# Tying the large products of a hybrid DeltaNet and mixture-of-experts block in program order, with three smaller moves

## The chip, the cores and the metric

The kernel runs on one core of a Trainium2 chip. The metric is the device time of one launch in microseconds (us). Engines are named as in the profile: PE is TensorE (matmul), PEld its weight load, DVE is VectorE, ACT is ScalarE, POOL is GpSimd, SP is SyncE, which issues nearly all DMA.

## The reference, cut to what matters

One block of a decoder over 512 tokens of width 1024, in float32:

```python
proj = x @ w_in                                  # q, k, v, z, a, b, uv, two gates
q, k, v = split(silu(causal_conv4(qkv)))         # 8 heads of 128; q and k are normalised
beta = sigmoid(b)
g = -exp(a_log) * softplus(a + dt_bias)          # per token and head, summed along the tokens
o = gated_delta_rule(q, k, v, g, beta)           # decay = exp(g_cum differences), triangular solves, state
y_dn  = (rms_norm(o) * silu(z)) @ w_dn_out
y_sgu = (u * (W_causal @ layer_norm(v_sgu) + b)) @ w_sgu_out
y = (sigmoid(gate_dn) * y_dn + sigmoid(gate_sgu) * y_sgu) @ w_out
h = layer_norm(ALPHA * x + y)
# router: the best of 4 groups, 2 of its 4 experts, combine weights
ffn = sum_e combine_e * ((silu(h @ w_gate_e) * (h @ w_up_e)) @ w_down_e)     # 16 experts, FF 256
out = layer_norm(ALPHA * h + ffn)
```

## The kernel before

**Split products.** Nearly every product is made of three: each float32 operand is split into a high half (a copy rounded to float32r, made by ACT) and a low half (what is left, made by DVE with a subtraction that waits for the copy). `mm3` (L235 to L237) issues high x high, high x low, low x high into one PSUM bank, 512 columns each. Three lines are thus the bulk of PE's work: L235, L236 and L237 in the projections, L1202 to L1204 in the experts.

**Blocks.** `chan_tile` makes one block of 24 such products (8 chunks of the contraction by 3) for 128 channels by 512 tokens. `tok_half` makes half a block for 128 tokens by 512 channels. The results lie in PSUM tiles `pa`, of which there are four, taken in turn. The small products (transposes, attention, the state) use four tiles `pb`.

**Weights.** `wload` fetches one MB of weights into one of three raw buffers, lets ACT make the high half (L149) in one of two buffers, and DVE the low half in place of the raw data (L150). One load serves two `chan_tile` blocks.

**The start.** x comes in four pieces; `xturn(k)` transposes chunk k of it on PE (L224 is the warm up, L230 the transposes), ACT writes its high half (L231), DVE its low half (L232). The first half of z's projection is multiplied as x arrives: `z_first(w, kh, m)` does two of the eight chunks for four token tiles. Then come the projections a and b (16 columns), the gates made of them (L323 to L356: Exp, Ln and the cumulative sums on PE, L342 and L343), and the rest of z.

**The heads.** For each of 8 heads of k: a block, a convolution (ACT L384, three DVE steps L386, ACT Silu L387), the small products k k^T (L414), and on DVE their norms (L416) and the matrix A (L400). The decay matrix DM is fetched through DRAM (L363 stores the cumulative gate, L405 reads it back, broadcast), masked by POOL (L425), shifted by DVE (L427) and put through Exp by ACT (L428). Then q with the other half of z, a forward substitution on DVE, v, the recurrence over four chunks of tokens, u, the spatial gate, the merge (L748 to L759), the output projection, the router.

**The experts.** For each expert e the loop does `gate_up(e + 1)` (24 products), the turn of the next tokens (L1180, L1182, L1183), the split of later weights (`esplit`: ACT L809, DVE L813), the transposes of the hidden rows (L1304) with their two halves (ACT L1305, DVE L1307), and `down(e)`. Of the four quarters of `down`, three are made of three split products each. The fourth (n = 1, f = 1) is one product of whole float32 operands: `FHF`, an unsplit copy of the hidden rows made by ACT (L1306), times the unsplit weights (L1224). So the last quarter of each down weight isn't split.

**What sets the order.** A scheduler places the instructions of each engine in a fixed list before the kernel runs. It follows data dependences and, among what it takes for ready, program order; its idea of when something is ready is its own. `K(...)` pins an instruction behind the one traced before it on its engine. `tc.issue_after(ins)` puts those instructions of its block that are on the engine of `ins` behind `ins` in the list; it adds no wait on other engines. The blocks of the projections are not pinned: their products are placed in any order between blocks, though in order within one. The expert loop is pinned throughout. At run time each engine goes through its list in order.

Of the kernel before, what the change touches and what calls it, by code (L numbers as in the profile page):

```python
# [21 lines left out]
NT = 4  # L22
H = 8
KT = 8
# [12 lines left out]
def body(ctx: ExitStack, tc: tile.TileContext, P: dict, out):  # L37
# [161 lines left out]
    xload(2)  # L199
    SP.dma_start(wab, w_in[:, COLS["ab"]:COLS["ab"] + 16].rearrange("(k p) n -> p k n", p=128))  # L200
    fz.append(wfetch(whalf(w_z, 0, 1), 2))
# [32 lines left out]
    def mm3(o, lh, ll, rh, rl, first, last, pin=lambda ins: ins):  # L234
        pin(T.matmul(o, lh, rh, start=first, stop=False))  # L235
        pin(T.matmul(o, lh, rl, start=False, stop=False))  # L236
        pin(T.matmul(o, ll, rh, start=False, stop=last))  # L237

    def chan_tile(w, j, rh=None, rl=None, pin=lambda ins: ins):

        whi, wlo = w
        p = pa()
        for k in range(KT):
            mm3(p, whi[:, k, j * 128:(j + 1) * 128], wlo[:, k, j * 128:(j + 1) * 128],
                XHI[:, k, :] if rh is None else rh(k), XLO[:, k, :] if rl is None else rl(k),
                k == 0, k == KT - 1, pin)
        return p

    def tok_half(p, w, i, kh, lh=None, ll=None, cs=slice(0, 512), pin=lambda ins: ins, ks=range(4)):

        whi, wlo = w
        ts = slice(i * 128, (i + 1) * 128)
        for k in ks:
            mm3(p, (XHI if lh is None else lh)[:, kh * 4 + k, ts], (XLO if ll is None else ll)[:, kh * 4 + k, ts],
                whi[:, k, cs], wlo[:, k, cs], kh + k == 0, kh == 1 and k == 3, pin)
# [22 lines left out]
    def z_first(w, kh, m):  # L278

        for i in range(NT):  # L280
            tok_half(pz[i], w, i, kh, pin=K, ks=range(2 * m, 2 * m + 2))
# [9 lines left out]
    for k in range(4, KT):  # L291
        xturn(k)
    split(wab, wabl, wabh, V, K)
    w = wload(None, fz[1], K)
    z_first(w, 1, 0)
# [32 lines left out]
    A.activation(sl, su, AF.Ln)  # L328
# [16 lines left out]
    for i in range(NT):  # L345
        z_use(0)(i, pz[i])
# [5 lines left out]
    A.activation(Gc, gc, AF.Exp)  # L352
    A.activation(GL, gl, AF.Exp)
    V.tensor_scalar(nG, Gc, -1.0, None, op0=ALU.mult)
    V.tensor_tensor(kd, gl, gc, ALU.subtract)
    A.activation(kd, kd, AF.Exp)  # L356
# [49 lines left out]
    for h in range(H):  # L406
# [15 lines left out]
        if h == 1:  # L422
            for c in range(NT):
                with tc.issue_after(silu.ins):
                    G.affine_select(out=DM[:, c], in_=DM[:, c], compare_op=ALU.is_ge, fill=NEG, base=0,  # L425
                                    pattern=[[0, 8], [1, 128]], channel_multiplier=-1)
                    V.tensor_tensor(DM[:, c], DM[:, c], ngc[:, :, c, None].to_broadcast([128, H, 128]), ALU.add)  # L427
                    A.activation(DM[:, c], DM[:, c], AF.Exp)  # L428
        if h > 1:
            a_matrix(h - 2)  # L430
# [363 lines left out]
    def esplit(n, later=False):  # L794


# [7 lines left out]
        if part < 2:  # L804
            cuts = [lambda t: t[:, 0:2], lambda t: t[:, 2:4]]
        else:
            cuts = [lambda t: t[:, 0], lambda t: t[:, 1, 0:512]]
        for cut in cuts:
            K(A.activation(cut(hi), cut(raw), AF.Copy))  # L809

        def rest():
            for cut in cuts:
                K(V.tensor_tensor(cut(lo), cut(raw), f_(cut(hi)), ALU.subtract))  # L813
# [349 lines left out]
    FHF = cst(128)  # L1163
# [53 lines left out]
    def down(e, n):  # L1217
# [3 lines left out]
        for f in range(2 - n):  # L1221
            kmm3(p, FHH[:, f], FHL[:, f], wh[:, f, ns], wl[:, f, ns], f == 0, f == 1)
        if n == 1:
            K(T.matmul(p, FHF, raws[(e, 2)][0][:, 1, ns], start=False, stop=True))  # L1224
# [68 lines left out]
    for e in range(NE):  # L1293
# [12 lines left out]
        K(A.activation(FHF, p[:, 128:256], AF.Copy))  # L1306
# [125 lines left out]
```

## Time and profile before

| what | us |
|---|---|
| median of 3 runs (lowest, highest) | 836.5 (834.26, 838.26) |
| the profiled execution, its own time | 833.55 |
| its span, from first to last instruction | 831.8 |
| PE busy in the span | 787.8 (95%) |
| DVE, ACT, POOL busy | 522.8, 382.6, 106.1 |
| mean granted clock of PE | 0.978 |

The span is that of one profiled execution; 1.75 us of its time lie outside the span. A matmul's busy time overlaps that of the next one, so the distance between the starts of two matmuls is what one of them costs. Idle time of PE, and time at a granted clock of half, are what can be won on PE.

### The profile page before, as it was taken

Reading aid. Unit: us, or ns where it says so; the run is one execution under the profiler, and the core shown is the slowest. Engines: PE = TensorE matmul, PEld = TensorE weight load, DVE = VectorE, ACT = ScalarE, POOL = GpSimd, SP = SyncE. Lnnn points to the kernel's source line nnn. Section 1 sums busy time; section 2 is a strip of 40 time slices with the busy share of each in tenths; the row PEclk is TensorE's granted clock in tenths of the full one; section 3 lists DMA queues with packets and bytes.
Section 4 is the critical chain, followed back from the end, with each engine's and each line's share of the span. In section 5 each row is a group of like instructions: output and inputs, shape, how many; then the busy total and the mean of one; then the engine's idle time right before and its main releaser. Section 6 shows DMA issues by size and latency. Waiting matters only on the chain. (4 is left out here: it accounts for less than half of the span.)

```text
span 831.8 us, 10884 instructions
## 1 busy us (share of the span) xinstructions
PE 787.8 (95%) x4043; PEld 647.6 (78%) x4043; DVE 522.8 (63%) x1026; ACT 382.6 (46%) x629; POOL 106.1 (13%) x92
## 2 busy tenths in 40 slices
PE   8888999999999999999999999999995999999991
PEld 7577888787889988888788888888664777777771
DVE  3336882997575992447623233324469898889977
ACT  2395353453335543323322222222234888888843
POOL 0002002001100000001501000000032211110177
PEclk9998999999999999999999999999997999999997
DMA  9426336336260135243244333379718899998762
GB/s 223 87 63 157 85 79 142 85 71 153 49 134 2 52 77 100 81 102 97 102 110 98 101 101 102 102 274 335 249 52 267 287 382 390 369 336 294 290 244 101
DMA packets 110752, 133.65 MB, mean 161 GB/s; under 512 B 19780, under 2 KB 93032, under 8 KB 110696
## 3 DMA queue, kind: packets, MB, share of 16 engines
q1 hardware_dynamic: 107240, 120.33, 49.8%
q0 software_dynamic: 3456, 12.58, 4.2%
q8 instruction: 33, 0.54, 0.3%
q14 instruction: 23, 0.19, 0.1%
HBM read 120.82 MB, written 12.08 MB: 160 GB/s over the span
## 5 line engine op out<-in xcount | busy, mean ns | idle before, releaser
L235 PE MATMUL pa<-r,r 128*128 128x512 f32 (+1 forms) x712 | 280.6, 394 | 5.1 <-ACT r L149 4.9
L236 PE MATMUL pa<-r,r 128*128 128x512 f32 (+1 forms) x712 | 279.6, 393 | 2.7 <-DVE r L150 2.7
L237 PE MATMUL pa<-r,r 128*128 128x512 f32 (+1 forms) x712 | 278.5, 392 | 0.0
L150 DVE TENSOR_TENSOR r<-r,r 128x2048 fp32r<-128x2048 f32 (+2 forms) x48 | 102.0, 2131 | 132.4 <-ACT r L149 132.3
L235 PEld LDWEIGHTS pa<-r,r 128*128 128x128 f32 x712 | 134.9, 189 | 32.7 <-ACT r L149 5.7
L236 PEld LDWEIGHTS pa<-r,r 128*128 128x128 f32 x712 | 135.0, 190 | 30.2 <-DVE r L150 3.6
L237 PEld LDWEIGHTS pa<-r,r 128*128 128x128 f32 x712 | 135.2, 190 | 27.8 <-DVE r L232 0.4
L149 ACT ACTIVATE r<-r 128x2048 fp32r<-128x2048 f32 (+2 forms) x48 | 84.8, 1777 | 141.8 <-PE pa L236 83.4
L813 DVE TENSOR_TENSOR r<-r,r 128x1024 fp32r<-128x1024 f32 x96 | 108.8, 1134 | 13.1 <-ACT r L809 11.6
L809 ACT ACTIVATE r<-r 128x1024 fp32r<-128x1024 f32 x96 | 89.2, 983 | 0.0
L1202 PE MATMUL pa<-r,r 128*128 128x512 f32 x176 | 77.3, 439 | 0.3 <-ACT r L1182 0.3
L1204 PE MATMUL pa<-r,r 128*128 128x512 f32 x176 | 69.4, 395 | 0.0
L1203 PE MATMUL pa<-r,r 128*128 128x512 f32 x176 | 69.0, 392 | 0.0
L386 DVE SCALAR_TENSOR_TENSOR r<-pa,r,r 128x511 f32<-128x511 f32 (+2 forms) x72 | 53.5, 743 | 16.7 <-ACT r L384 16.2
L1202 PEld LDWEIGHTS pa<-r,r 128*128 128x128 f32 x176 | 33.1, 188 | 9.3 <-ACT r L809 1.9
L1203 PEld LDWEIGHTS pa<-r,r 128*128 128x128 f32 x176 | 33.2, 189 | 9.0 <-issue 3.1
L1204 PEld LDWEIGHTS pa<-r,r 128*128 128x128 f32 x176 | 33.0, 188 | 7.8 <-DVE r L1307 0.3
L387 ACT ACTIVATE r<-r 128x512 f32<-128x512 f32 x24 | 15.1, 631 | 46.4 <-DVE r L386 42.7
L758 POOL TENSOR_TENSOR r<-r,r 128x512 f32<-128x512 f32 x8 | 12.4, 1556 | 144.0 <-DVE r L757 137.3
L384 ACT ACTIVATE r<-pa,r 128x512 f32<-128x512 f32 x24 | 16.3, 680 | 26.9 <-PE pa L237 26.9
L1040 POOL DMA_INDIRECT r<-hD,r x16 | 17.3, 1080 | 87.7 <-PE pb L1180 45.9
L1182 ACT ACTIVATE r<-pb 128x512 fp32r<-128x512 f32 x32 | 19.1, 599 | 16.0 <-PE pb L1180 14.8
(328 smaller groups left out, 934.2 us busy)
## 6 DMA issues: line engine op xcount, KB each, us to landing
r<-in_w_in_dram SPq DMA_DIRECT2D x29, 1024.0 KB, 8.9
r<-in_expert_w_gate_dram SPq DMA_DIRECT2D x32, 512.0 KB, 5.9
r<-in_expert_w_down_dram SPq DMA_DIRECT2D x16, 1024.0 KB, 10.5
r<-in_expert_w_up_dram SPq DMA_DIRECT2D x32, 512.0 KB, 9.2
yD<-r SPq DMA_DIRECT2D x12, 512.0 KB, 8.7
r<-in_x_dram SPq DMA_DIRECT2D x8, 512.0 KB, 3.7
r<-in_w_dn_out_dram SPq DMA_DIRECT2D x4, 1024.0 KB
r<-in_w_sgu_out_dram SPq DMA_DIRECT2D x4, 1024.0 KB
```

The source lines that it names most:

```text
L149: pin(A.activation(hi, raw, AF.Copy))
L150: pin(eng.tensor_tensor(lo, raw, f_(hi), ALU.subtract))
L235: pin(T.matmul(o, lh, rh, start=first, stop=False))
L236: pin(T.matmul(o, lh, rl, start=False, stop=False))
L237: pin(T.matmul(o, ll, rh, start=False, stop=last))
L386: V.scalar_tensor_tensor(acc[:, s:], p[:, :S - s], wc(3 - s), acc[:, s:], op0=ALU.mult, op1=ALU.add)
L809: K(A.activation(cut(hi), cut(raw), AF.Copy))
L813: K(V.tensor_tensor(cut(lo), cut(raw), f_(cut(hi)), ALU.subtract))
L1182: K(A.activation(XGH[:, hs], v3(p), AF.Copy))
L1202: K(T.matmul(args[0], args[1], args[3], start=args[5], stop=False))
L1203: K(T.matmul(args[0], args[1], args[4], start=False, stop=False))
L1204: K(T.matmul(args[0], args[2], args[3], start=False, stop=args[6]))
```

## The change

Four edits. (1) `mm3` remembers its last product in `big`, and `chan_tile` and `tok_half` put their products behind it, so that the large products of one block follow all those of the block traced before. (2) The start of z: `z_first` runs through its products by term, high x high for all four tiles, then low of x, then low of the weights; its second half is moved ahead of the last two transposed chunks of x; the small load of the weights of a and b goes behind the second piece of z's weights. (3) The four Silu of z are put behind the Ln of the gates, and three Exp of the gates (Gc, GL, kd) move to the block in which DM goes through Exp. (4) The fourth quarter of `down` is made like the other three, so `esplit` splits the whole down weight, and the unsplit copy FHF is gone.

```diff
@@ the loads at the start
     xload(2)
+    fz.append(wfetch(whalf(w_z, 0, 1), 2))
     SP.dma_start(wab, w_in[:, COLS["ab"]:COLS["ab"] + 16].rearrange("(k p) n -> p k n", p=128))
-    fz.append(wfetch(whalf(w_z, 0, 1), 2))
@@ mm3, chan_tile, tok_half
-        pin(T.matmul(o, ll, rh, start=False, stop=last))
+        big[0] = pin(T.matmul(o, ll, rh, start=False, stop=last)).ins
+
+    big = [None]
+
+    def after_big():
+
+        return tc.issue_after(big[0]) if big[0] is not None else contextlib.nullcontext()
...
-        for k in range(KT):
-            mm3(p, whi[:, k, j * 128:(j + 1) * 128], wlo[:, k, j * 128:(j + 1) * 128],
...
+        with after_big():
+            for k in range(KT):
+                mm3(p, whi[:, k, j * 128:(j + 1) * 128], wlo[:, k, j * 128:(j + 1) * 128],
...
-        for k in ks:
-            mm3(p, (XHI if lh is None else lh)[:, kh * 4 + k, ts], (XLO if ll is None else ll)[:, kh * 4 + k, ts],
...
+        with after_big():
+            for k in ks:
+                mm3(p, (XHI if lh is None else lh)[:, kh * 4 + k, ts], (XLO if ll is None else ll)[:, kh * 4 + k, ts],
...
@@ z_first
-        for i in range(NT):
-            tok_half(pz[i], w, i, kh, pin=K, ks=range(2 * m, 2 * m + 2))
+        hi, lo = w
+        terms = ((XHI, hi), (XLO, hi), (XHI, lo))
+        for t, (x, y) in enumerate(terms):
+            for i in range(NT):
+                for k in range(2 * m, 2 * m + 2):
+                    K(T.matmul(pz[i], x[:, kh * 4 + k, i * 128:(i + 1) * 128], y[:, k, 0:512],
+                               start=kh + k + t == 0, stop=False))
@@ the order at the start
     z_first(w, 0, 1)
-    for k in range(4, KT):
+    for k in range(4, 6):
+        xturn(k)
+    w = wload(None, fz[1], K)
+    z_first(w, 1, 0)
+    for k in range(6, KT):
         xturn(k)
     split(wab, wabl, wabh, V, K)
-    w = wload(None, fz[1], K)
-    z_first(w, 1, 0)
     w_k0 = wload(None, f_k0, K)
@@ the gates
-    A.activation(sl, su, AF.Ln)
+    ln_ = A.activation(sl, su, AF.Ln)
...
-    for i in range(NT):
-        z_use(0)(i, pz[i])
+    with tc.issue_after(ln_.ins):
+        for i in range(NT):
+            z_use(0)(i, pz[i])
...
-    A.activation(Gc, gc, AF.Exp)
-    A.activation(GL, gl, AF.Exp)
-    V.tensor_scalar(nG, Gc, -1.0, None, op0=ALU.mult)
     V.tensor_tensor(kd, gl, gc, ALU.subtract)
-    A.activation(kd, kd, AF.Exp)
@@ head 1 of k, behind the Exp of DM
+            with tc.issue_after(silu.ins):
+                A.activation(Gc, gc, AF.Exp)
+                A.activation(GL, gl, AF.Exp)
+                A.activation(kd, kd, AF.Exp)
+                V.tensor_scalar(nG, Gc, -1.0, None, op0=ALU.mult)
@@ esplit
-        if part < 2:
-            cuts = [lambda t: t[:, 0:2], lambda t: t[:, 2:4]]
-        else:
-            cuts = [lambda t: t[:, 0], lambda t: t[:, 1, 0:512]]
-        for cut in cuts:
-            K(A.activation(cut(hi), cut(raw), AF.Copy))
+        halves = (slice(0, 2), slice(2, 4)) if part < 2 else (slice(0, 1), slice(1, 2))
+        for s in halves:
+            K(A.activation(hi[:, s], raw[:, s], AF.Copy))
...
@@ down and the expert loop
-        for f in range(2 - n):
+        for f in range(2):
             kmm3(p, FHH[:, f], FHL[:, f], wh[:, f, ns], wl[:, f, ns], f == 0, f == 1)
-        if n == 1:
-            K(T.matmul(p, FHF, raws[(e, 2)][0][:, 1, ns], start=False, stop=True))
...
         K(A.activation(FHH, v3(p[:, 0:256]), AF.Copy))
-        K(A.activation(FHF, p[:, 128:256], AF.Copy))
```

## Rows read from the trace of the kernel before

**Rows 1.** The page's first two parts: busy time, share of the span and instructions of PE, then the span in 40 equal slices (20.8 us each): busy tenths of PE and DVE, and the granted clock of PE.

```profile
PE 787.8 (95%) x4043; PEld 647.6 (78%) x4043; DVE 522.8 (63%) x1026; ACT 382.6 (46%) x629; POOL 106.1 (13%) x92
PE   8888999999999999999999999999995999999991
DVE  3336882997575992447623233324469898889977
PEclk9998999999999999999999999999997999999997
```

**Rows 2.** Busy time of each engine by stretch (us from the span's start: length, then busy us and instructions of PE, PEld, DVE, ACT, POOL, then granted clock, DMA share, GB/s).

```profile
28.00:55.00 27.00, 27.00 (x117) 19.65 (x118) 6.11 (x19) 15.80 (x23) 0.00 (x0) 0.94 0.24 44
55.00:78.00 23.00, 18.09 (x73) 14.39 (x72) 15.49 (x31) 13.49 (x15) 5.21 (x4) 0.85 0.62 172
78.00:125.00 47.00, 47.00 (x238) 39.39 (x237) 40.60 (x134) 21.41 (x29) 0.00 (x0) 1.00 0.33 80
404.00:560.00 156.00, 156.00 (x690) 129.17 (x689) 51.86 (x43) 40.51 (x38) 15.43 (x10) 1.00 0.43 128
641.00:804.00 163.00, 162.43 (x765) 128.84 (x766) 145.57 (x189) 132.23 (x206) 25.51 (x23) 0.99 0.95 333
```

**Rows 3.** The waits of PE: line that waited, what ended the wait, us in total, times, longest.

```profile
PE pa L235 <- ACT r L149: 4.9, 3, 2.7
PE pa L236 <- DVE r L150: 2.7, 3, 1.1
PE pb L414 <- ACT r L387: 2.2, 1, 2.2
PE pb L488 <- ACT r L387: 1.1, 1, 1.1
```

**Rows 4.** Timeline of PE, and of ACT, in the start (start us, us, engine, line, operation, shapes, count, idle before and its releaser).

```profile
8.92 0.50 PE L235 MATMUL pa<-r,r 128*128 128x512 f32 x1 [0.17 <-ACT r L149]
10.18 0.50 PE L236 MATMUL pa<-r,r 128*128 128x512 f32 x1 [0.76 <-DVE r L150]
22.70 1.91 PE L230 MATMUL pb<-r,r 128*128 128x128 f32 x16
26.59 0.50 PE L235 MATMUL pa<-r,r 128*128 128x512 f32 x1 [1.98 <-ACT r L149]
34.69 0.40 PE L235 MATMUL pb<-r,r 128*16 128x512 f32 x1
23.34 2.06 ACT L231 ACTIVATE r<-pb 128x512 fp32r<-128x512 f32 x4 [6.07 <-PE pb L230]
25.26 4.12 ACT L149 ACTIVATE r<-r 128x128 fp32r<-128x128 f32 x5
```

**Rows 5.** The gates: a transfer of a's products to DVE, the table loads of ACT in 40 to 56 us (grouped by line: count, busy us, mean ns), and PE's product behind z's last ones.

```profile
42.18 0.19 DVE L323 TENSOR_TENSOR r<-pb,r 128x32 f32<-128x32 f32 x1 [10.89 <-PE pb L311]
L273 ACT ACT_TABLE_LOAD x4 | 5.1, 1283 | 0.1
52.23 0.27 PE L359 MATMUL pb<-r,r 128*32 128x128 f32 x1
```

**Rows 6.** The first heads of k, timelines of PE, ACT, DVE and POOL.

```profile
58.51 0.40 PE L236 MATMUL pa<-r,r 128*128 128x512 f32 x1
61.63 0.66 PE L235 MATMUL pa<-r,r 128*128 128x512 f32 x1 [2.72 <-ACT r L149]
71.60 1.70 PE L414 MATMUL pb<-r 128*128 128x128 f32 x8 [2.19 <-ACT r L387]
55.69 1.91 ACT L149 ACTIVATE r<-r 128x2048 fp32r<-128x2048 f32 x1
55.82 2.32 DVE L386 SCALAR_TENSOR_TENSOR r<-pa,r,r 128x511 f32<-128x511 f32 x3 [2.91 <-ACT r L384]
58.05 2.28 DVE L150 TENSOR_TENSOR r<-r,r 128x2048 fp32r<-128x2048 f32 x1
66.32 1.23 DVE L427 TENSOR_TENSOR r<-r,r 128x1024 f32<-128x1024 f32 x1 [5.33 <-POOL r L425]
104.25 2.26 DVE L150 TENSOR_TENSOR r<-r,r 128x2048 fp32r<-128x2048 f32 x1
```

**Rows 7.** Busy time by stretch again, in the heads of k (columns as in rows 2).

```profile
55.80:61.00 5.20, 3.11 (x14) 2.22 (x12) 5.11 (x5) 3.82 (x3) 0.00 (x0) 1.00 0.41 129
66.30:106.50 40.20, 38.01 (x184) 31.59 (x183) 34.84 (x112) 17.67 (x20) 4.11 (x3) 0.96 0.42 104
```

**Rows 8.** One pass of the expert loop: its busy time (columns as in rows 2), then timelines of PE and DVE, and last a group of lines in the experts (count, busy us, mean ns).

```profile
701.52:711.08 9.56, 9.56 (x47) 7.58 (x46) 8.49 (x11) 8.43 (x14) 1.15 (x1) 1.00 1.07 376
700.65 1.02 PE L1224 MATMUL pa<-r,r 128*128 128x512 f32 x2
701.75 0.40 PE L1203 MATMUL pa<-r,r 128*128 128x512 f32 x1
701.41 1.95 DVE L813 TENSOR_TENSOR r<-r,r 128x1024 fp32r<-128x1024 f32 x2
704.33 2.48 DVE L813 TENSOR_TENSOR r<-r,r 128x1024 fp32r<-128x1024 f32 x2 [0.97 <-ACT r L809]
706.73 0.42 DVE L1307 TENSOR_TENSOR r<-pb,r 128x256 fp32r<-128x256 f32 x1
L1234 DVE SCALAR_TENSOR_TENSOR r<-pa,r,r 128x512 fp32r<-128x512 f32 x4 | 2.8, 744 | 0.0
```

More of the change, by code (lines that the diff above doesn't have):

```diff
@@ L1 @@
+import contextlib
 import math
@@ L242, in chan_tile @@
         p = pa()
-        for k in range(KT):
-            mm3(p, whi[:, k, j * 128:(j + 1) * 128], wlo[:, k, j * 128:(j + 1) * 128],
-                XHI[:, k, :] if rh is None else rh(k), XLO[:, k, :] if rl is None else rl(k),
-                k == 0, k == KT - 1, pin)
+        with after_big():
+            for k in range(KT):
+                mm3(p, whi[:, k, j * 128:(j + 1) * 128], wlo[:, k, j * 128:(j + 1) * 128],
+                    XHI[:, k, :] if rh is None else rh(k), XLO[:, k, :] if rl is None else rl(k),
+                    k == 0, k == KT - 1, pin)
         return p
@@ L252, in tok_half @@
         ts = slice(i * 128, (i + 1) * 128)
-        for k in ks:
-            mm3(p, (XHI if lh is None else lh)[:, kh * 4 + k, ts], (XLO if ll is None else ll)[:, kh * 4 + k, ts],
-                whi[:, k, cs], wlo[:, k, cs], kh + k == 0, kh == 1 and k == 3, pin)
+        with after_big():
+            for k in ks:
+                mm3(p, (XHI if lh is None else lh)[:, kh * 4 + k, ts], (XLO if ll is None else ll)[:, kh * 4 + k, ts],
+                    whi[:, k, cs], wlo[:, k, cs], kh + k == 0, kh == 1 and k == 3, pin)
     def tok_group(src, cg, use):
@@ L803, in esplit @@
         ready[order[n]] = hi, lo
-        if part < 2:
-            cuts = [lambda t: t[:, 0:2], lambda t: t[:, 2:4]]
-        else:
-            cuts = [lambda t: t[:, 0], lambda t: t[:, 1, 0:512]]
-        for cut in cuts:
-            K(A.activation(cut(hi), cut(raw), AF.Copy))
+        halves = (slice(0, 2), slice(2, 4)) if part < 2 else (slice(0, 1), slice(1, 2))
+        for s in halves:
+            K(A.activation(hi[:, s], raw[:, s], AF.Copy))
         def rest():
-            for cut in cuts:
-                K(V.tensor_tensor(cut(lo), cut(raw), f_(cut(hi)), ALU.subtract))
+            for s in halves:
+                K(V.tensor_tensor(lo[:, s], raw[:, s], f_(hi[:, s]), ALU.subtract))
         if later:
@@ L1162, in body @@
     FHH = cst(2, 128, dt=F32R)
-    FHF = cst(128)
     FHL = carve(mixer_only, (2, 128), F32R)[0]
```

## The prediction

> **What bounds the kernel now.** I read the page's slices first: PE is at 9 tenths in 34 of 40 slices, nearly throughout at its full granted clock [rows 1]. The stretches say where it isn't: between 404 and 560 us PE is busy in every microsecond at clock 1.00, in the experts (641 to 804) in 162.43 of 163 [rows 2]. There only work taken off PE can shorten the time. The page's low slices near 630 us (the router) and at the end hold nothing that the change touches. What is left are PE's waits: 4.9 us for a high half (ACT L149), 2.7 for a low half (DVE L150), 2.2 for a Silu ahead of L414 [rows 3]. By the timelines most of them lie in the start [rows 4] and in the first heads of k, 55 to 78 us [rows 6], where PE is busy 18.09 of 23 us at a granted clock of 0.85 [rows 2]. PE is the bound, and the change can pay in these two places and in the expert loop. I sum against the profiled execution's 833.55 us; the median of the runs shown, 836.5, is 2.95 above it, which I add at the end.
>
> **The start.** A large product costs 0.23 us (690 instructions, nearly all of them large products, fill the 156 us from 404 to 560 [rows 2]). Before, the second product of z waited for the low half: 10.18 - 8.92 = 1.26 in place of 0.23 [rows 4]. By term, 16 products (3.7 us) run before the first that reads a low half, which was there at 10.1: 1.0 us won, and the second quarter of z ends near 21.5, not 22.7. Before, all four transposed chunks came next, ACT copied four (2.06 us), then the a, b weights, then z's next high half, and PE went on at 26.59 [rows 4]. After the change only two chunks stand ahead: the copies start 0.64 after the transposes (23.34 - 22.70), take 1.1, the high half 1.1 (the 4.12 us of L149 hold four of these and the narrow one [rows 4]): PE goes on at 24.3. It does 24 products (5.5) to 29.8, two chunks of transposes to 30.9, then waits for their copies and the narrow a, b high half (0.3): the products of a and b begin at 32.0 and lose 0.4 more to the low half, against 34.69. Won: 2.4. An idle 1.9 us remains at 22.4; the like wait before was followed by slow products (28 to 55 at a clock of 0.94: 1.6 us [rows 2]). If that comes again it takes 1.6 back; this is the lower bound. The a, b load lands later by one piece of weights, over 10 us ahead of its split: nothing.
>
> **The gates.** Tied, head 0 can no longer be done between the parts of z, as it was (its 24 products lie ahead of 52.23 [rows 5]). So PE reaches the cumulative product 5.4 us sooner after z's parts, and g must be there. From L323 at 42.18, in times of before: some nine small steps of 0.2 (0.19 in the row) on DVE and ACT, and one table load of 1.28, for Ln: 45.2 [rows 5]. PE, with 12 products after the transposes that L323 waits for, is there at 42.1 + 2.8 = 44.9. A wait of 0.3. Start and gates together: 2.1 won, at worst 0.5.
>
> Table loads there fall from eight to two (four of the eight are L273's, 1283 ns each [rows 5]), 7.7 us off ACT. They are not on PE's path, but what ACT does next is. The Trainium skill ("ScalarE: Activation LUTs", section "What ACT_TABLE_LOAD costs") gives 2.66 us for a switch, a drain included. Here four loads take 5.1 us with 0.1 idle before them, so the trace doesn't bear that out; by the page the wait for g would be 1.7 in place of 0.3, and the whole gain 1.4 smaller.
>
> **The heads of k.** Before, PE stopped at 58.74 (58.51 + 0.23) until 61.63, waiting for a high half [rows 6]. The row at 58.51 is a second product (L236) and the next a first one (L235), not a third: the list had gone on to a block whose weights weren't there. What the block at hand lacked, its low half, was made from 58.05 to 60.33; its split had begun at 55.69 on ACT, behind the table loads [rows 6]. Tied, and with ACT free: z's last product ends at 52.23 - 2.4 - 5.4 + 0.3 = 44.7, the Silus at 45.6, the split at 47.5 on ACT and 49.8 on DVE, and its first block begins when head 1 ends: 44.7 + 2 x 5.45 = 55.6. This wait (2.9 us) goes. The second, of 2.2, is for head 1's Silu: DVE did one step of its convolution and then stood 5.33 us before L427, which waited for POOL and the decay matrix from DRAM [rows 6]. Around both the clock fell: 23 us at 0.85 [rows 2] cost 3.45. Together PE loses 8.6 us there, 10.7 with the start: the upper bound.
>
> What is late next is DVE. The low half that ends at 106.5, the fourth wide one from 58.05 on, is for the first block of q [rows 6]. Up to it DVE was busy 5.11 us from 55.8 to 61.0, not at all to 66.3, then 34.84 of 40.2 [rows 6, 7]: 39.95 us of work from its first convolution on, which all comes ahead of that low half in its list. After: head 0's block ends at 44.7 + 5.4 = 50.1, its convolution begins 1.1 later on DVE (copy on ACT between): 51.2 in place of 55.82. If all of DVE's idle time stayed, 4.6 would be won; if it went, more than PE's 10.7. The decay matrix takes 14.1 us from L359 to L427 (66.32 - 52.23), so L427 could start at 58.8, when the first step of head 1's convolution ended at 57: of 5.3 idle 2.0 stay. The other 5.4 (40.2 less 34.84) I keep, as waits on ACT and PE in a fixed list. 51.2 + 39.95 + 5.4 + 2.0 = 98.5 against 106.5: **8.0 us won** from the start to here, bounds 4.6 and 10.7. After that the lead carries on, since what follows is PE's (slices at 9 [rows 1]).
>
> **After the heads.** The tie changes nothing in PE's sum where it is always busy [rows 2]. The waits for L488 (1.1 [rows 3]) and the like may go or come; taken as nothing, between -2 and +4.
>
> **The experts.** The unsplit product and a split one take 701.75 - 700.65 = 1.10 [rows 8], less 0.23: 0.87. Three split ones take 0.69. 0.18 for each of 16 experts: 2.8 us off PE, a pass of 9.38. ACT copies 512 columns more, 0.5 by the copies of 512 in the start (2.06 / 4 [rows 4]), and drops FHF: at most 8.9. DVE's pair on the down weight goes from 1.95 to 2.48 as the other pairs are, +0.53: 9.02 of 9.38 [rows 8]. Its one gap, 0.97 before the pair of 2.48, is the cover; were it not there, the pass would be DVE's. DVE's chain then starts some 0.6 later in the pass. L1307 ended at 707.15 and PE reads it near 708.5 (26 large and ten small products after 701.52): 0.7 is left in hand. From expert 12 on DVE also does two steps of 744 ns [rows 8], about 1.3: PE waits once, some 0.5. **2.3 won**, bounds 0 and 2.8.
>
> **Sum.** 833.55 - 8.0 - 2.3 = 823.2; with 2.95 for the median of the runs, **826 us**.
>
> **Rivals.** (a) DVE loses its idle time in the heads, and PE gets all of 10.7: 823.5. For it: those gaps are waits on blocks that now come sooner. Against: DVE was busy 34.84 of 40.2 with PE slower. (b) DVE keeps all its idle time, the 5.3 too: 4.6 + 2.3 won, 829.6. For it: the list put L427 inside the convolution before. (c) The tie doesn't do what it says, as the second weights' split is again late in ACT's list: the wait at 58 stays, 2.1 + 2.3 are won, 832. Against: little else is ready on ACT at 45.6. (d) DVE becomes the bound of the experts: 9.02 a pass plus gaps. From gaps of 0.54 (9.56 - 9.02) the gain there is gone; if the pass came to 10.4, 14 passes would lose 11.8, less 8.0: 840. (e) **Slower:** with products tied, PE has less to put between a block and the small products behind its Silu (L414, L488 and their like, 24 groups). Each waits for a copy, three DVE steps (2.32 [rows 6]) and a Silu, 4 to 5 us in all, with one block of 5.4 between. Where the list places them too soon, PE stands and nothing overtakes. Two such waits cost 2.2 and 1.1 before [rows 3], 1.65 on average. From 0.43 a group (10.3 / 24) the gain is gone; at 1.65 for 15 of the 24 it costs 25, and the time is 851. Against it: from 78 to 125, with DVE busy 40.60 of 47, PE never stood [rows 2].
>
> **How the numbers follow.** Chances: my sum 0.42, (a) 0.18, (b) 0.14, (c) 0.10, (d) 0.05, (e) 0.11. Half a per cent (4.2 us) is about what runs of this kernel can tell from no change (three spread over 4.0), so faster is below 832.3, slower above 840.7. Faster: my sum and (a), 0.11 of (b), half of (c): 0.76. Same: 0.03 of (b), half of (c), (d): 0.13. Slower: (e), 0.11. My sum's own range, from its bounds, is 822 to 831. The range for 8 in 10 takes in (a) with waits of the middle gone, and (b) to (d) in part: 816 to 838.
>
> **What would show it.** Right: PE's first product of a and b near 32; two table loads between 40 and 46; PE without a stop of over 1 us from 45 to 70 and no half clock there; the first convolution on DVE near 51; passes of 9.4 with DVE's gap near 0.4; one wait for L1307's work near the end. Wrong: PE's waits for Silu or low halves add up to more than 5 us between 50 and 200, DVE idle for 5 us before L427, or passes above 9.56.

## The result, and the profile after

The change made the kernel slower: 840.35 us median of 9 runs (836.77 to 842.78) against 834.26 for the kernel before (9 runs, 831.23 to 838.26). The ratio is 1.007, interval 1.0049 to 1.009. The profiled execution took 839.72 us, its span is 838.0. Lines up to about L230 move down by one; L163 is now the fetch of weights, L150 and L151 their high and low halves, L236 to L238 the products of `mm3`, L294 those of `z_first`, L397, L399 and L400 the convolution's copy, steps and Silu, L427 the small products of k, L429 their norms, L376 the store of the cumulative gate, L418 the readback of the decay matrix, L438 its mask, L440 its shift, L441 its Exp, L506 the small products of q, L1317 the low half of the hidden rows.

The first two parts of the profile's page, as in [rows 1]:

```profile
PE 783.0 (93%) x4059; PEld 647.5 (77%) x4059; DVE 535.4 (64%) x1026; ACT 376.6 (45%) x606; POOL 110.9 (13%) x92
PE   8896799999999999999999999999995999999991
DVE  3437873797666894339633332323658899999987
PEclk9997899999999999999999999999998999999996
```

PE's slices sink to 6 and 7 in the fourth and fifth, 63 to 105 us, where they were 8 and 9. The stretches of [rows 2] say how much:

```profile
28.00:55.00 27.00, 25.30 (x118) 17.65 (x116) 11.16 (x24) 12.44 (x20) 0.00 (x0) 1.00 0.34 70
55.00:78.00 23.00, 15.02 (x68) 12.56 (x68) 13.60 (x27) 6.75 (x7) 6.11 (x4) 0.82 0.53 137
78.00:125.00 47.00, 42.05 (x201) 34.89 (x200) 36.85 (x126) 18.47 (x26) 0.00 (x0) 0.90 0.27 68
404.00:560.00 156.00, 154.01 (x695) 127.67 (x695) 56.21 (x49) 40.54 (x40) 21.62 (x14) 1.00 0.39 114
641.00:804.00 163.00, 153.91 (x771) 126.70 (x771) 155.48 (x216) 138.68 (x194) 29.59 (x24) 0.97 0.95 334
```

From 55 to 125 us PE loses 12.93 us of busy time, against 4.91 before, and the granted clock is 0.82 and 0.90 where it was 0.85 and 1.00. The last two rows hold no new loss: the stretches are fixed, the kernel is about 8 us later in them, so PE's wait of 5.4 us ahead of the experts, which before lies in front of 641 us, now falls inside, as does one of 1.9 that lay in front of 404. Of PE's waits (columns of [rows 3]), two in the heads of k are long:

```profile
PE pb L427 <- ACT r L400: 8.0, 1, 8.0
PE pa L238 <- DVE r L151: 6.5, 2, 4.9
PE pa L294 <- ACT r L150: 3.0, 2, 1.7
PE pb L506 <- ACT r L400: 1.6, 1, 1.6
PE pa L1217 <- DVE r L1317: 1.0, 2, 0.6
```

The timelines of SP, POOL, DVE and PE (columns of [rows 4]) show where the first one comes from:

```profile
45.32 0.37 SPq L163 DMA_DIRECT2D r<-in_w_in_dram  x1
45.97 0.34 SPq L376 DMA_DIRECT2D gcd<-r  x1
55.19 5.33 SPq L418 DMA_DIRECT2D r<-gcd  x4
60.46 1.09 POOL L438 TENSOR_SCALAR_AFFINE_SELECT r<-r 128x1024 f32<-128x1024 f32 x1 [59.19 <-DMA r<-gcd]
51.94 2.32 DVE L399 SCALAR_TENSOR_TENSOR r<-pa,r,r 128x511 f32<-128x511 f32 x3 [1.65 <-ACT r L397]
61.59 1.23 DVE L440 TENSOR_TENSOR r<-r,r 128x1024 f32<-128x1024 f32 x1 [7.34 <-POOL r L438]
67.36 2.97 DVE L151 TENSOR_TENSOR r<-r,r 128x2048 fp32r<-128x2048 f32 x1
70.33 0.74 DVE L399 SCALAR_TENSOR_TENSOR r<-pa,r,r 128x511 f32<-128x511 f32 x1
59.20 0.67 ACT L397 ACTIVATE r<-pa,r 128x512 f32<-128x512 f32 x1
32.03 0.41 PE L236 MATMUL pb<-r,r 128*16 128x512 f32 x1 [0.94 <-ACT r L150]
75.08 2.08 PE L427 MATMUL pb<-r 128*128 128x128 f32 x8 [7.98 <-ACT r L400]
96.70 2.29 DVE L151 TENSOR_TENSOR r<-r,r 128x2048 fp32r<-128x2048 f32 x1
```

DVE ends head 0's convolution at 54.25 and stands until 61.59: next in its list is the first shift of the decay matrix, which POOL could mask only from 60.46 on, when it was back from DRAM. Head 1's convolution has had its copy since 59.87 (the row of ACT at 59.20) and could have gone then. It stands behind three shifts and the low half of the third group's weights, begins at 70.33, and its Silu lets PE go at 75.08. So of the 10.46 us from 59.87 to 70.33 DVE's wait for the first shift is 1.72; the rest is what the list has between. The last row is what PE's second wait, of 4.9 us, is for: the fourth group's low half, made as late as 96.70 to 98.99. In the kernel before one of head 1's three steps stood ahead of the first shift, and 5.33 us of idle ahead of it [rows 6].

The next table sets all the kernels of this study beside before; those other than after are explained in the next section. Weighing each large product with 0.23 us and each small one with 0.11, I read off when PE has done the same amount of work in two traces. A column's entry is the time at which the kernel gets there less that of before, in us (before does 50 us of work by 66.2, 60 by 80.1, 80 by 100.7, 200 by 223.7, 470 by 508.6):

| kernel | ratio, interval | 50 | 60 | 80 | 200 | 470 |
|---|---|---|---|---|---|---|
| after | 1.0070 (1.0049 to 1.0090) | -6.0 | +0.6 | +7.9 | +9.6 | +8.4 |
| z_only | 0.9955 (0.9934 to 0.9977) | -3.8 | -2.6 | -2.6 | -2.6 | -2.6 |
| gates_only | 1.0094 (1.0063 to 1.0125) | -4.9 | -0.6 | +5.4 | +6.2 | +6.2 |
| tie_only | 1.0145 (1.0119 to 1.0171) | +3.0 | +8.8 | +13.7 | +15.3 | +14.0 |
| exp_only | 0.9983 (0.9957 to 1.0010) | -1.4 | -1.6 | -1.6 | -2.4 | -3.7 |
| z_exp | 0.9960 (0.9941 to 0.9979) | +1.1 | -1.5 | -1.4 | -1.5 | -2.8 |
| no_tie | 1.0051 (1.0031 to 1.0071) | -5.8 | -0.5 | +7.3 | +8.1 | +6.8 |
| dm_first | 0.9975 (0.9954 to 0.9996) | +3.4 | -0.4 | +0.1 | +1.8 | +1.8 |
| dm_after | 0.9957 (0.9936 to 0.9978) | -5.6 | -9.4 | -3.2 | -2.4 | -3.6 |
| dm_after_notie | 0.9924 (0.9898 to 0.9950) | -6.1 | -10.0 | -6.2 | -5.3 | -5.3 |
| dm_notie_noexp | 0.9940 (0.9918 to 0.9962) | -6.0 | -9.9 | -6.3 | -5.3 | -5.3 |
| gates_dm | 0.9974 (0.9953 to 0.9995) | -2.3 | -6.1 | -0.8 | +0.1 | +0.1 |
| tie_dm | 1.0030 (1.0004 to 1.0056) | +3.7 | +0.5 | +1.9 | +1.6 | +2.8 |
| pe_later | 1.0100 (1.0071 to 1.0129) | -5.9 | -9.9 | +7.4 | +8.3 | +7.0 |
| rb_first | 0.9947 (0.9923 to 0.9971) | -0.1 | -4.0 | -3.5 | -1.8 | -1.8 |
| lo_notie | 0.9859 (0.9834 to 0.9884) | -6.0 | -9.8 | -8.7 | -6.1 | -7.4 |
| lo_tie | 0.9894 (0.9868 to 0.9920) | -5.8 | -9.0 | -8.0 | -8.2 | -8.8 |

Each ratio is against runs of before on the same chip. The columns are single executions: exp_only stands at -3.7 ahead of the code that it edits, so only jumps larger than that, or rows that agree, are read from them. So after gains 6 us by the first 50 us of work, gives 6.6 back by 60 (the first wait and the time at half the clock behind it), and 7.3 more by 80 (the second).

### The profile page after: what moved, and what is told of

It reads as the page before. It is cut to its first block, busy times and chain, and to the rows that moved or that the text cites. A ratio compares the mean times of both kernels' runs of the same rounds, so it can differ in the third digit from the quotient of the medians.

```text
span 838.0 us, 10893 instructions
## 1 busy us (share of the span) xinstructions
PE 783.0 (93%) x4059; PEld 647.5 (77%) x4059; DVE 535.4 (64%) x1026; ACT 376.6 (45%) x606; POOL 110.9 (13%) x92
## 5 line engine op out<-in xcount | busy, mean ns | idle before, releaser
L238 PE MATMUL pa<-r,r 128*128 128x512 f32 (+1 forms) x688 | 269.0, 391 | 6.5 <-DVE r L151 6.5
L236 PE MATMUL pa<-r,r 128*128 128x512 f32 (+1 forms) x688 | 270.5, 393 | 0.0
L237 PE MATMUL pa<-r,r 128*128 128x512 f32 (+1 forms) x688 | 269.1, 391 | 1.1 <-DVE r L151 1.1
L151 DVE TENSOR_TENSOR r<-r,r 128x2048 fp32r<-128x2048 f32 (+2 forms) x48 | 102.9, 2147 | 138.5 <-ACT r L150 138.1
L238 PEld LDWEIGHTS pa<-r,r 128*128 128x128 f32 x688 | 130.0, 189 | 33.4 <-DVE r L151 7.4
L237 PEld LDWEIGHTS pa<-r,r 128*128 128x128 f32 x688 | 130.1, 189 | 26.8 <-DVE r L151 1.5
L236 PEld LDWEIGHTS pa<-r,r 128*128 128x128 f32 x688 | 130.2, 189 | 25.8 <-ACT r L150 0.2
L150 ACT ACTIVATE r<-r 128x2048 fp32r<-128x2048 f32 (+2 forms) x48 | 84.8, 1774 | 134.2 <-PE pa L237 80.6
L827 DVE TENSOR_TENSOR r<-r,r 128x1024 fp32r<-128x1024 f32 x96 | 117.1, 1222 | 5.1 <-ACT r L823 2.9
L823 ACT ACTIVATE r<-r 128x1024 fp32r<-128x1024 f32 x96 | 96.4, 1059 | 0.0
L1215 PE MATMUL pa<-r,r 128*128 128x512 f32 x192 | 77.8, 405 | 0.2 <-ACT r L1195 0.2
L1217 PE MATMUL pa<-r,r 128*128 128x512 f32 x192 | 75.8, 395 | 1.0 <-DVE r L1317 1.0
L1216 PE MATMUL pa<-r,r 128*128 128x512 f32 x192 | 75.4, 392 | 0.0
L399 DVE SCALAR_TENSOR_TENSOR r<-pa,r,r 128x509 f32<-128x509 f32 (+2 forms) x72 | 53.3, 744 | 12.8 <-ACT r L397 11.9
L1217 PEld LDWEIGHTS pa<-r,r 128*128 128x128 f32 x192 | 36.0, 188 | 9.9 <-DVE r L1317 1.9
L1215 PEld LDWEIGHTS pa<-r,r 128*128 128x128 f32 x192 | 36.1, 188 | 7.3 <-ACT r L1195 0.5
L1216 PEld LDWEIGHTS pa<-r,r 128*128 128x128 f32 x192 | 36.2, 188 | 6.9
L400 ACT ACTIVATE r<-r 128x512 f32<-128x512 f32 x24 | 15.1, 631 | 55.4 <-DVE r L399 52.6
L1054 POOL DMA_INDIRECT r<-hD,r x16 | 20.5, 1284 | 84.2 <-PE pb L1193 42.5
L397 ACT ACTIVATE r<-pa,r 128x512 f32<-128x512 f32 x24 | 16.4, 682 | 33.8 <-PE pa L238 33.7
```

The costliest lines, as they stand in the source:

```text
L150: pin(A.activation(hi, raw, AF.Copy))
L151: pin(eng.tensor_tensor(lo, raw, f_(hi), ALU.subtract))
L238: big[0] = pin(T.matmul(o, ll, rh, start=False, stop=last)).ins
L399: V.scalar_tensor_tensor(acc[:, s:], p[:, :S - s], wc(3 - s), acc[:, s:], op0=ALU.mult, op1=ALU.add)
L823: K(A.activation(hi[:, s], raw[:, s], AF.Copy))
L827: K(V.tensor_tensor(lo[:, s], raw[:, s], f_(hi[:, s]), ALU.subtract))
```

## The experiments

**The four edits one by one.** Each kernel is before with the hunks of one edit of the diff above: gates_only the gates and head 1 of k, tie_only `mm3`, `chan_tile` and `tok_half`, z_only the loads, `z_first` and the order at the start, exp_only `esplit`, `down` and the expert loop. In short:

```diff
 gates_only
+    with tc.issue_after(ln_.ins):
+        for i in range(NT):
+            z_use(0)(i, pz[i])
...
+                A.activation(Gc, gc, AF.Exp)
 tie_only
+        with after_big():
+            for k in range(KT):
+                mm3(p, whi[:, k, j * 128:(j + 1) * 128], wlo[:, k, j * 128:(j + 1) * 128],
 z_only
+        for t, (x, y) in enumerate(terms):
 exp_only
+        for f in range(2):
+            kmm3(p, FHH[:, f], FHL[:, f], wh[:, f, ns], wl[:, f, ns], f == 0, f == 1)
```

> The kernel before with the gates' edit alone: z's Silus behind the Ln, the exponentials of Gc, GL and kd inside the decay block. In this kernel VectorE's list has the first shift of the decay matrix ahead of all three convolution steps of the second head of k, as the kernel after has it, and in the kernel before only behind the first step. Theory 1 (the loss comes from that place in VectorE's list, whichever edit brings it about): VectorE stands from the end of the first head's convolution (about 56) until the decay matrix is back from DRAM (about 60), TensorE then stands 5 to 9 us before the second head's small products, and a half clock follows; time before + 4 to + 10 us, ratio 1.005 to 1.012. Theory 2 (the loss comes from the tie, since TensorE has nothing to overtake with): no loss here, the two table loads less give back 0 to 2 us, ratio 0.997 to 1.000.

> The kernel before with the tie of the large products alone. Here too VectorE's list has all four shifts of the decay matrix ahead of the second head's convolution steps, though the gates are as before. Theory 1: a standstill of TensorE of 5 to 9 us near 70 us, time before + 4 to + 10 us (ratio 1.005 to 1.012), and the one of 4.9 us at 58 on the second group's weights stays or goes with the list. Theory 2 (the tie itself): + 6 to + 11 us as well, and then gates_only shows nothing; the two runs together tell the theories apart. Theory 3 (neither; the loss is in the experts): 0.999 to 1.001.

> The kernel before with the start alone: z's products by term, the second half's weights fetched and split earlier. VectorE's list through the heads of k is that of the kernel before. All theories: the small products of a and b begin some 2.4 us earlier, near 32.2 instead of 34.7; whether the gain lasts is open: theory 1 says it lasts in part, since no list changes behind it, time before - 1 to - 3 us, ratio 0.996 to 0.999; theory 4 (the start only shifts the wait to the second group's weights at 58, which land by the DMA's clock): 0.999 to 1.001, with that wait longer by about 2.

> The kernel before with the experts' edit alone: the whole low half of the down weights split on VectorE, six products of two terms in place of five and a full float product. Theories 1 and 2: a gain of 2 to 6 us in the experts, less up to 3 in the tail, time before - 1 to - 5 us, ratio 0.994 to 0.999. Theory 3 (VectorE's longer split, or the tail behind the last expert, costs more than TensorE gains): ratio 1.001 to 1.006.

The gates' edit alone costs 0.94%, with no tie in the kernel. Its DVE and PE rows are those of after, a little earlier:

```profile
60.99 1.23 DVE L424 TENSOR_TENSOR r<-r,r 128x1024 f32<-128x1024 f32 x1 [5.65 <-POOL r L422]
69.88 0.74 DVE L383 SCALAR_TENSOR_TENSOR r<-pa,r,r 128x511 f32<-128x511 f32 x1
74.64 2.08 PE L411 MATMUL pb<-r 128*128 128x128 f32 x8 [6.44 <-ACT r L384]
97.85 0.50 PE L237 MATMUL pa<-r,r 128*128 128x512 f32 x1 [2.90 <-DVE r L150]
```

DVE idle ahead of the first shift, head 1's convolution from 69.88, PE standing 6.44 for its Silu, then 2.90 for the fourth group's low half. The tie alone costs 1.45%, 12.9 us by the medians, more than any theory had: the same standstill of 7.1 us, and besides 4.3 us of its own earlier, which tied products can't fill while the gates' work is late (the waits of PE):

```profile
PE pb L423 <- ACT r L396: 7.1, 1, 7.1
PE pa L238 <- DVE r L151: 5.0, 2, 3.4
PE pb L351 <- DVE r L344: 4.3, 1, 4.3
```

The start alone gains 2.8 us by the medians, within the 1 to 3 expected, and keeps it: -2.6 us from the 60th us of work on. exp_only can't be told from no change. Theory 2, that the tie is what costs, doesn't stand as told: gates_only loses without it. What gates_only, tie_only and after have in common, and z_only and before have not, is the place of the shifts in DVE's list.

**Undoing the tie, and putting the shifts back.** no_tie is after without the hunks of the tie. dm_after is after with the shifts kept behind head 1's last convolution step; dm_after_notie the same without the tie; z_exp is before with the start's and the experts' edits.

```diff
     for s in (1, 2, 3):
-        V.scalar_tensor_tensor(acc[:, s:], ...)
+        cv[0] = V.scalar_tensor_tensor(acc[:, s:], ...)
...
-                with tc.issue_after(silu.ins):
+                with tc.issue_after(silu.ins), tc.issue_after(cv[0].ins):
                     G.affine_select(out=DM[:, c], ...)
```

> The kernel after without the tie: z's products by term, the gates' edit and the experts' edit stay. VectorE's list through the heads of k is still that of the kernel after (the decay matrix's first shift ahead of the second head's three convolution steps). Theory 1 (that place in the list costs, with or without the tie): the sum of the single parts, gates + 8 us, start - 3, experts - 1, gives time before + 4 us, ratio 1.002 to 1.007, with TensorE standing 5 to 9 us for the second head's Silu. Theory 2 (the tie costs): the loss is gone, ratio 0.992 to 0.998.

> The kernel after, with one thing more: VectorE's four shifts of the decay matrix are kept behind the last convolution step of the second head. The list becomes: first head's convolution, its norms, the split of the third group's low half, second head's convolution, then the shifts. Theory 1: the standstill of 8 us at 67 goes, and with it the half clock behind it; the later one of 5 us (low half of a group of k's weights late on VectorE) shrinks too, since VectorE no longer stands from 54 to 61; time after - 8 to - 14 us, ratio to before 0.989 to 0.997. Theory 2 (the tie costs, by leaving TensorE nothing to go on with): another wait takes the place, ratio 1.000 to 1.006.

> The same order on VectorE as in dm_after, without the tie. Theory 1: within 2 us of dm_after, ratio 0.988 to 0.997. Theory 2: well below dm_after, by 4 us or more.

> The kernel before with the start's and the experts' edits, without the tie and the gates' edit: VectorE's list through the heads of k stays that of the kernel before. Theory 1: the two single gains add, - 2.8 and - 1.2 us, ratio 0.993 to 0.997, faster than the kernel before and than the kernel after by some 10 us. Against it would be 0.998 or more: then one gain is taken back by the other's place.

Without the tie the loss stays (1.0051), as theory 1 had it. With the shifts behind the convolution it turns into a gain, tied (0.9957) or not (0.9924). Untied is better here by 2.4 us: ten of the twelve runs of dm_after lie above all six of dm_after_notie, on the same chip. The -9.4 and -10.0 us at 60 us of work show the first standstill gone whole. In dm_after, stretch, DVE's and PE's rows:

```profile
55.00:78.00 23.00, 22.49 (x110) 18.30 (x109) 19.44 (x50) 14.81 (x18) 6.02 (x4) 1.00 0.72 180
62.11 2.31 DVE L401 SCALAR_TENSOR_TENSOR r<-pa,r,r 128x511 f32<-128x511 f32 x3
88.81 0.79 PE L238 MATMUL pa<-r,r 128*128 128x512 f32 x1 [3.42 <-DVE r L151]
```

Head 1's convolution begins at 62.11 in place of 70.33, and PE is busy 22.49 of 23 us at full clock. What remains is a wait for the fourth group's low half: 3.42 tied; untied it is 0.87 for the high half and 1.36 for the low one. z_exp (0.9960) has the start's gain, and of the experts' nothing that shows in the medians.

**Is it the place in the list alone?** dm_first leaves before as it is and keeps head 1's steps behind the third shift.

```diff
+            for c in range(NT):
+                G.affine_select(out=DM[:, c], ...)
+                sh.append(V.tensor_tensor(DM[:, c], DM[:, c], ngc..., ALU.add))
+            with tc.issue_after(sh[2].ins):
+                silu = conv_silu(p, 8 + h, KTr[:, h])
```

> The kernel before, and only the place of one step moved: the second head's convolution steps are kept behind the third shift of the decay matrix on VectorE (none of the change's parts is in it). Theory 1 (that place costs by itself): VectorE waits near 60 for the decay matrix from DRAM, TensorE then stands some 5 to 9 us for the second head's Silu; time before + 5 to + 10 us, ratio 1.006 to 1.012, as gates_only. If it costs nothing (0.998 to 1.002), the place in the list is not the cause and goes only along with it.

This one missed: 0.9975, no loss. Its rows:

```profile
64.08 0.80 PE L235 MATMUL pa<-r,r 128*128 128x512 f32 x1 [4.86 <-ACT r L149]
68.77 1.23 DVE L415 TENSOR_TENSOR r<-r,r 128x1024 f32<-128x1024 f32 x1 [2.41 <-POOL r L413]
77.11 0.74 DVE L386 SCALAR_TENSOR_TENSOR r<-pa,r,r 128x511 f32<-128x511 f32 x1
81.40 1.16 PE L423 MATMUL pb<-r 128*128 128x128 f32 x8 [0.36 <-ACT r L387]
```

Head 1's convolution begins even later, at 77.11. But PE stood 4.86 us at 64 for the third group's high half, whose weights landed late in this execution (ACT's copy waited 3.10 us for them, 0.96 in before), went on at half the clock, and its list had 91 large products between g's cumulative sum and head 1's small ones, where before has 56 and after 96. It came to them at 81.40, just when they were ready. And DVE's idle time was about the 5.33 of before: 3.45 ahead of the second of the two low halves that the list put in between, 2.41 ahead of the shift. So a late place of the convolution by itself need not cost. This reading rests on one trace, and that execution took 2.4 us more than the kernel's median. It left open whether DVE's list, PE's list or the late readback is to be held for the loss, and four more runs went to that.

**Which list, or the readback.** gates_dm and tie_dm are gates_only and tie_only with the edit of dm_after. pe_later is after with DVE's list the same through the shifts and head 1's steps, and with head 1's small products behind the blocks of the next three heads. rb_first is after with the third group's fetch behind the readbacks on SP.

```diff
 pe_later
+        if h == 1:
+            w1 = wload(wcol("k", 1))
+            ahead[2], ahead[3] = chan_tile(w1, 0), chan_tile(w1, 1)
+            w = wload(wcol("k", 2))
+            ahead[4] = chan_tile(w, 0)
...
+            with after_big() if h == 1 else contextlib.nullcontext():
                 T.matmul(p[:, c * 128:(c + 1) * 128], kc, kc, start=True, stop=True)
 rb_first
-        SP.dma_start(DM[:, c], src)
+        rb = SP.dma_start(DM[:, c], src)
...
+            if h == 4:
+                with tc.issue_after(rb.ins):
+                    f_k2 = wfetch(wcol("k", 2))
```

> gates_only with one thing more: VectorE's four shifts of the decay matrix behind the second head's convolution. If the loss of gates_only (+ 8 us) is that place in the list, it goes: TensorE's standstills at 68 to 74.6 and at 95 to 98 are gone or small, and the ratio to before is 0.994 to 1.000. If the gates' edit costs in another way (exponentials, table loads), it stays at 1.004 or more.

> tie_only with the same order on VectorE. The standstill of 7 us at 76 to 83 should go, and that of 3.4 us at 102; what tie_only has of its own, 4.3 us at 46 to 51 in which TensorE waits for g's cumulative sum with a half clock before it, stays: time before + 1 to + 6 us, ratio 1.001 to 1.007. If the tie costs through the heads themselves, as I had it among the rivals of the prediction, it stays at 1.010 or more.

> The kernel after with VectorE's list as it is (decay matrix ahead of the second head's convolution), but the second head's small products behind the large ones of the next three heads in TensorE's list: 126 large products after the cumulative sum instead of 96, some 7 us. Theory A (the loss is the meeting of the two lists: TensorE reaches the small products at 67 while their Silu comes at 74 to 75): the standstill of 8 us goes or shrinks below 2, ratio to before 0.995 to 1.003. Theory B (VectorE's late work is what is lost, wherever TensorE meets it): TensorE stands at the next place that needs VectorE or a free bank, ratio 1.004 to 1.010.

> The kernel after with the third group of k's weights fetched behind the decay matrix's four readbacks on SP's queue instead of ahead of them. Nothing is left out. If VectorE's wait for the decay matrix (54.3 to 61.6) comes from the 1 MB fetch that stands ahead of it, the readbacks land some 6 us earlier, VectorE's shifts are done by about 60, and the standstill at 67 goes: ratio to before 0.990 to 0.999. In this kernel's list the shifts stand between the first head's convolution steps, so if the readbacks still land near 60, even the first head's small products wait: ratio 1.006 or more.

gates_dm: from 1.0094 to 0.9974, and tie_dm: from 1.0145 to 1.0030, by 1.2 and 1.1% with the one edit. pe_later: 1.0100, theory B. It is 9.9 us ahead at 60 us of work, past the place where after stands, and 7.4 behind at 80; PE's rows:

```profile
80.52 2.08 PE L434 MATMUL pb<-r 128*128 128x128 f32 x8 [5.62 <-ACT r L400]
91.98 1.16 PE L434 MATMUL pb<-r 128*128 128x128 f32 x8 [1.84 <-ACT r L400]
96.65 2.08 PE L434 MATMUL pb<-r 128*128 128x128 f32 x8 [3.51 <-ACT r L400]
```

PE's standstill only moves to the next places that need a convolution: what DVE loses by its idle time (5.00 ahead of the shift here) and by its order PE meets further on. rb_first gains 0.5% over before, 1.2% over after, with no pin on DVE:

```profile
45.94 0.32 SPq L376 DMA_DIRECT2D gcd<-r  x1
48.40 6.17 SPq L418 DMA_DIRECT2D r<-gcd  x4
53.87 1.09 POOL L441 TENSOR_SCALAR_AFFINE_SELECT r<-r 128x1024 f32<-128x1024 f32 x1 [52.59 <-DMA r<-gcd]
54.99 1.22 DVE L443 TENSOR_TENSOR r<-r,r 128x1024 f32<-128x1024 f32 x1 [2.34 <-POOL r L441]
63.76 0.75 DVE L399 SCALAR_TENSOR_TENSOR r<-pa,r,r 128x511 f32<-128x511 f32 x1
```

With no megabyte ahead of the store, the readbacks are issued 2.5 us after it, not 9.2, and POOL's mask runs at 53.87, not 60.46. All four shifts still stand ahead of head 1's convolution (63.76), and PE doesn't wait for it. But the scheduler ordered DVE anew too: two of the shifts stand between the steps of head 0's convolution, and PE waits 3.2 us (57 to 60) for head 0's small products; and the low half of the third group, which took 2.97 us ahead of head 1's convolution in after, now stands behind it (67.19). So this run shows that the shifts may stand ahead if the data is early; how much of the gain is the data's and how much the low half's it doesn't tell. The cause then is DVE's list: head 1's convolution behind shifts that wait for the decay matrix from DRAM. To move the shifts mends it by itself (dm_after, gates_dm, tie_dm); to bring the data earlier mended it together with a new order. Why the scheduler's list changes with the gates or with the tie, and not with the start, no run shows.

**The second standstill, and the experts' share.** lo_notie and lo_tie add to dm_after_notie and dm_after that the fourth group's weights are split ahead of the later decay products; dm_notie_noexp is dm_after_notie with the experts of before.

```diff
+        if h == 4:
+            nxt = wload(wcol("k", 3), None, lo_.append)
...
-        if h > 1:
+        if h > 3:
+            with tc.issue_after(lo_[-1].ins):
+                a_matrix(h - 2)
+        elif h > 1:
             a_matrix(h - 2)
```

> dm_after_notie with one thing more: the weights of k's fourth group are split before the products of the decay matrix with k times k of the third head and later ones, so that their low half stands earlier in VectorE's list. If TensorE's remaining waits near 85 to 88 us (0.9 and 1.4 us in dm_after_notie) are for that low half alone, they go: dm_after_notie - 1 to - 3 us, ratio to before 0.988 to 0.993. If VectorE is simply full there, the wait moves to the next convolution or small product: within 1 us of dm_after_notie, 0.991 to 0.995.

> dm_after, tied, with the same early split of the fourth group. If the tie costs only by leaving TensorE no work while that low half is late (3.4 us at 85 in dm_after, against 2.2 in two parts without the tie, and less clock behind it), tied and untied come out alike: within 1 us of lo_notie, ratio 0.988 to 0.994. If the tie costs otherwise, it stays 2 to 4 us over lo_notie.

> dm_after_notie with the experts of the kernel before. From the profiles an expert takes 9.57 us in the kernel before and 9.39 in the kernel after: 16 of them make 2 to 3 us, so dm_after_notie + 2 to + 3 us, ratio to before 0.994 to 0.997. If the split of the whole low half on VectorE gives nothing at the end (the tail loses it again): within 1 us of dm_after_notie, 0.991 to 0.994.

lo_notie is the best version of the study: 823.07 us against 834.21, ratio 0.9859. Its stretches from 55 to 78 and from 78 to 125 (columns of [rows 2]):

```profile
55.00:78.00 23.00, 22.48 (x109) 18.21 (x108) 19.83 (x52) 14.89 (x18) 5.58 (x4) 1.00 0.71 178
78.00:125.00 47.00, 46.74 (x238) 39.44 (x238) 34.83 (x113) 20.35 (x35) 1.89 (x2) 1.00 0.36 82
```

PE is busy 46.74 of 47 us. So the second standstill was the low half's place. Tied it gains as much against dm_after (0.9894 from 0.9957). Whether the tie costs anything once both are mended stays open: by the medians 2.4 us, as in the pair of dm_after, but of six and four runs with intervals that overlap, while the profiled spans go the other way (821.7 tied, 824.1 untied). dm_notie_noexp lies 0.16% over dm_after_notie, 1.3 us, less than the 2 to 3 expected and less than runs on two chips can tell.

## Why the prediction was wrong, point by point

**Start.** Right. a and b's products begin at 32.03 (32.0 forecast), and PE is 2.3 us ahead at 30 us of work (2.4 forecast, though 34.69 less 32.0 and 0.4 makes 2.3). No half clock came back from 28 to 55 (1.00). z_only shows the gain lasting.

**Gates.** Right in size: PE waits 0.56 for g (0.3 forecast), with two table loads from 40 to 46, 1.28 each as in [rows 5], and the activation behind the first one began at 41.96, 0.02 after it. The Trainium skill ("ScalarE: Activation LUTs", section "What ACT_TABLE_LOAD costs") has the same 1.28 for the load and adds a drain, 2.66 in all; of that drain this trace shows nothing. The rows:

```profile
40.66 1.28 ACT L344 ACT_TABLE_LOAD   x1
42.20 1.28 ACT L282 ACT_TABLE_LOAD   x1
43.45 0.38 PE L358 MATMUL pb<-r,r 128*128 128x32 f32 x2 [0.56 <-DVE r L351]
```

What I didn't ask of this edit is what else it does to a list: by itself it moved three of the shifts ahead of head 1's steps (gates_only).

**Heads of k.** Right up to 66 us: the wait at 58 is gone (gates_only and tie_only have each lost it alone, z_only still has 2.73), the first convolution begins at 51.94 (51.2), PE is 6.0 ahead. The step that failed is "L427 could start at 58.8, when the first step of head 1's convolution ended at 57: of 5.3 idle 2.0 stay". It took DVE's list from the kernel before and only shifted it in time. In the list of after all three steps of head 1 stand behind three of the shifts, so the idle time was 7.34, not 2.0, and it lay ahead of work that PE needed. The 14.1 us from the gates to the first shift became 16.2 (45.36, the start of L372, to 61.59), since in this execution the readback was slow to start (the last section has its spread). The milestone I had chosen, q's first low half, was too far back to show it: it ended at 103.53, 3.0 ahead of before (8.0 forecast). In the terms of the sum, DVE began at 51.94 for 51.2, worked 36.02 us for 39.95, and stood 15.57 for 7.4: the 7.34, and another 8.2 where 5.4 was kept, in which it mostly waited for PE's small products (4.5) and ACT's copies (2.1), late themselves. Meanwhile the fourth group's low half, the one PE stood for, ended at 98.99 against 91.48 in before. Term: -8.0 forecast, +7.9 measured at 80 us of work; with DVE's order mended it is -8.0 tied (lo_tie) and -8.7 untied (lo_notie), inside the bounds of 4.6 and 10.7. That it meets the forecast is luck in part, since those kernels also move the fourth group's split, which the sum didn't have.

**After the heads.** +0.5 (from +7.9 to +8.4), inside -2 to +4.

**Experts.** Right in sign and inside the bounds, but smaller than the 2.3 forecast. From +8.4 at 470 us of work to +6.2 at the end of the span 2.2 are won, of which the experts hold only 1.4: from the first to the last large product of the experts before takes 167.4 us (646.44 to 813.86) and after 166.0 (654.73 to 820.76). All eight kernels without this edit take 167.4 there, and nine of the ten with it 166.0 to 166.4 (no_tie 167.4). ACT's copies of the hidden rows were 9.55 apart (704.70 to 714.25) and are 9.41 (9.38 forecast), DVE's gaps 0.24 and 0.27 (0.4), and the low half of the hidden rows makes PE wait twice, 1.0 in all (once, 0.5), about half of what is missing:

```profile
704.70 0.38 ACT L1305 ACTIVATE r<-pb 128x256 fp32r<-128x256 f32 x1 [0.41 <-PE pb L1304]
714.25 0.38 ACT L1305 ACTIVATE r<-pb 128x256 fp32r<-128x256 f32 x1 [0.40 <-PE pb L1304]
703.46 0.39 ACT L1316 ACTIVATE r<-pb 128x256 fp32r<-128x256 f32 x1
712.87 0.38 ACT L1316 ACTIVATE r<-pb 128x256 fp32r<-128x256 f32 x1
712.96 2.48 DVE L827 TENSOR_TENSOR r<-r,r 128x1024 fp32r<-128x1024 f32 x2 [0.27 <-DMA r<-in_expert_w_down_dram]
```

In the medians of exp_only and dm_notie_noexp a gain of this size doesn't rise above what the runs can tell.

**Sum.** The profiled execution took 839.72 us for 823.2: the heads have 15.9 of these 16.5. The 2.95 added for the median came from three runs; the median of nine, 834.26, lies 0.71 above the profiled execution of before, so 2.2 of the 826 were too much, which by chance brought the forecast nearer to the result.

**Rivals.** (e) named the sign and the symptom, a small product behind its Silu listed too soon; but it made the tie the cause and many waits of 1.65 the price. It was one wait of 8.0, with a late low half (4.9) behind it, and no_tie has that wait too, at 7.0. (a) and (b), more or less of DVE's idle time, asked the right question with the list held fixed. (c) and (d) did not occur.

## What to carry to other kernels

Where a scheduler lays out the lists, an edit of one engine's order can reorder another engine two stages on, as gates_only and tie_only show; a forecast that shifts the old list in time needs, for each instruction that waits on DRAM, the question what would stand behind it if it came first. Pin the consumers of a readback behind the work that feeds the busiest engine, and put the readback and its store ahead of bulk fetches on their queue. A gain in front of a wait for DRAM isn't kept while work for the busiest engine stands behind that wait: after, gates_only and no_tie came 5 to 6 us earlier to it and lost that there.

## What the runs showed of the hardware that I had not expected

A store of 16 KB (32x128 float32) issued 0.65 us behind a fetch of 1 MB on the same queue let its readback go 9.2 us later (45.97 to 55.19); without the fetch ahead, 2.5 us (rb_first, 45.94 to 48.40). In before the same fetch stood 0.64 us ahead and the readback went 7.0 us later (52.84 to 59.82); over the 17 traces with the fetch ahead it is 6.7 to 9.3, so after's is near the longest, and the 2.5 is one trace. A low half on DVE took 2.97 us at 67.36, where POOL's mask ran until 68.19, and 2.29 at 47.99 with POOL idle; what of this POOL does was not tried.
